# Where the tiles of x lie in SBUF: 2048 bytes apart in place of 2112, and one offset for the Strassen sums outside of them

## The chip, the core and the metric

The program runs on one core of a Trainium2 chip. The metric is the device time of one execution in microseconds (us). TensorE (PE in the profile) multiplies a stationary operand, loaded by LDWEIGHTS (PEld), with a moving operand that streams past it, and adds into PSUM. ScalarE (ACT) and VectorE (DVE) make its operands, SyncE (SP) issues most DMA transfers, GpSimd (POOL) does little here. SBUF is the on-chip memory of 128 partitions; an address below is a byte address inside each partition.

## The reference, cut to what matters

One decoder layer over 512 tokens of width 2048, batch 1, all in float32: a mixer of three head groups behind one input projection, cross-attention into 256 memory tokens, and a gated MLP (D_FF = 5504) with a causal depthwise convolution of width 3 on the gate. Before each stands an RMS norm, after each a residual add; a last RMS norm closes it.

```python
def hybrid_mixer(h, w_in, ...):
    proj = h @ w_in                       # (512, 2048) @ (2048, 6168)
    qa, ka, va, qb, kb, vb, fl, qc, kc, vc, rc, gl = jnp.split(proj, ...)
    o_a = dilated_mixture_attention(...)  # 12 heads of 64
    o_b = forgetting_attention(...)       # 8 heads of 64
    o_c = rms_norm(gla_chunked(...)) * jax.nn.silu(rc)
    return jnp.concatenate([o_a, o_b, o_c], axis=-1) @ w_out

def memory_cross_attention(h, mem_n, w_q, w_kv, w_o):
    ...                                   # 4 heads of 128, softmax over 256 memory tokens
    return o @ w_o

def conv_ffn(h, w_up, conv_w, conv_b, w_down):
    val, gate = jnp.split(h @ w_up, 2, axis=-1)
    g = conv_b
    for i in range(CONV_W):
        g = g + conv_w[i] * gp[:, i:i + S]
    return (jax.nn.silu(g) * val) @ w_down

def reference(x, mem, ...):
    mem_n = rms_norm(mem, mem_norm)
    for l in range(DEPTH):                # DEPTH = 1
        x = x + hybrid_mixer(rms_norm(x, norm_mix[l]), ...)
        x = x + memory_cross_attention(rms_norm(x, norm_cross[l]), mem_n, ...)
        x = x + conv_ffn(rms_norm(x, norm_ffn[l]), ...)
    return rms_norm(x, norm_final)
```

## The kernel before

Activations stand with features on the partitions and the 512 tokens along the row: 16 tiles of 128 x 512. Every float32 operand is split in two: ACT rounds it to fp32r ("hi"), DVE subtracts to get the rest ("lo"). A product is then three matmuls, hi with hi, lo of the moving operand with hi, hi with lo of the weights (`mm3`, lines 352 to 354). Weights come by DMA into `wraw` and are split into `whi` and `wlo`, tiles of 2048 bytes, of which a matmul takes 128 columns (512 bytes) as its stationary operand.

The work on PE goes stage by stage:

- the mixer's projections (`out_units`: the moving operand is a tile of x, 512 columns; `nat_units`, lines 393 to 395: the moving operand is a weight tile of 384, 408 or 512 columns, and 128 columns of a tile of x are the stationary one). After every 12 matmuls of `out_units`, `tick` may put in instructions of attention or of the gated linear attention, matmuls among them;
- the output projection `w_o`, the keys and values of the memory (`mhi`, `mlo`, 256 columns), and the cross-attention, whose output projection moves `coh` and `col` (512 columns);
- the up projection of the MLP, 43 rounds of seven Strassen products. Both factors are cut into quarters, so its moving operands are sums of quarters with 256 columns. `token_sums` makes 56 of them: eight pairs i = 0 to 7 by seven products. Each is one tile that holds hi (1024 bytes) and behind it lo (1024 bytes). A product runs over i = 0 to 7 in that order, three matmuls each, 24 in a row;
- the down projection: 43 tiles of the gate product g, 512 columns, of which some lie in the tiles of x (`xhi`, `xlo`) and some in tiles of their own (`gh`, `gl`, `gkh`, `gkl`); PE goes over them in blocks.

The tiles of x are 16 `xhi` and 16 `xlo` of the pool `xp` (`xslot`, line 292). They hold the normed x, then the mixed heads, then x again for the cross-attention, then the first 32 of the 56 sums (slots 0 to 31, that is i = 0 to 3 and four of i = 4), then tiles of g, then the last weights. The other 24 sums lie in pools of their own (`sx`, `fa`) and are named `sum32` to `sum55`.

Where they lie, in the program as built (the phase is the address modulo 512, since the slices of a weight tile stand 512 bytes apart):

| tiles | first address | distance | phase |
|---|---|---|---|
| whi, wlo | 32192, 42432 | 2048 | 448 |
| x tiles, before | 52672 | 2112 | 448, 0, 64, 128, ... (64 more each tile; `xhi` and `xlo` of one number have one phase) |
| mhi, mlo | 175040 | 1024 | 448 |
| coh, col | 153024 | 2048 | 448 |
| gh, gl | 168896, 189376 | 2048 | 448 |
| sum32 to sum48, before | 193408 | 2112 | 384, 448, 0, ... |
| sum49 to sum55, before | 153024 | 2112 | 448, 0, 64, ... |

Inside its tile a Strassen sum of pair i begins SHIFT[i] words behind the start: 0, 4, 8, 16, 24, 32, 48 or 56 bytes for i = 0 to 7. The order of the instructions is that of the code; pools place tiles one behind the other.

Of the kernel before, what the change touches and what calls it, by code (L numbers as in the profile page):

```python
# [13 lines left out]
F32R = mybir.dt.float32r  # L14
# [5 lines left out]
P = 128  # L20
D = 2048
KT = D // P
S = 512
# [22 lines left out]
FC = ((0, 5), (5, 10))  # L46
GX_SLOTS = 16
GB_SLOTS = 10
SHIFT = (0, 1, 2, 4, 6, 8, 12, 14)
LEVELS = (64, 32, 16, 8, 4, 2, 1)  # L50
A_PATTERNS = ((128, 1), (512, 4), (2048, 16))
REL_BUCKETS = 32
# [159 lines left out]
class _Trunk:  # L212
# [77 lines left out]
        return self.gains[:, i * KT + k:i * KT + k + 1]  # L290

    def xslot(self, n=S):
        hi = self.xp.tile([P, n], F32R, name="xhi", tag="xhi", bufs=KT, padded_shape=[P, S + 16])
        lo = self.xp.tile([P, n], F32R, name="xlo", tag="xlo", bufs=KT, padded_shape=[P, S + 16])
        return hi, lo

    def split(self, src, n=S):
# [835 lines left out]
    def token_sums(self, i, pool, tmp):  # L1133

        nc = self.nc
        y = []
        for e in range(2):
            t = tmp.tile([P, S], F32, name="y%d" % e, tag="y%d" % e, bufs=2)
            nc.scalar.activation(t, self.x1[2 * i + e], AF.Copy, scale=self.gain(2, 2 * i + e))
            y.append(t)  # L1140
        a11, a21 = y[0][:, :HT], y[0][:, HT:]
        a12, a22 = y[1][:, :HT], y[1][:, HT:]
        s = [tmp.tile([P, HT], F32, name="s%d" % n, tag="s%d" % n, bufs=2) for n in range(1, 5)]
        src = {1: a11, 6: s[1], 5: s[0], 7: s[2], 4: a22, 2: a12, 3: s[3]}
        made = {5: (a21, a22, ALU.add), 6: (s[0], a11, ALU.subtract), 7: (a11, a21, ALU.subtract),
                3: (a12, s[1], ALU.subtract)}
        out = {}
        for n, j in enumerate((1, 5, 6, 7, 4, 2, 3)):
            if j in made:
                nc.vector.tensor_tensor(src[j], made[j][0], made[j][1], op=made[j][2])  # L1150
            slot = 7 * i + n
            if slot < 2 * KT:
                tag = ("xhi", "xlo")[slot % 2]
                t = self.xp.tile([P, S + 16], F32R, name=tag, tag=tag, bufs=KT)
            else:
                t = pool.tile([P, S + 16], F32R, name="sum%d" % slot)
            o = SHIFT[i]
            th, tl = t[:, o:o + HT], t[:, o + HT:o + S]
            nc.scalar.activation(th, src[j], AF.Copy)  # L1159
            nc.vector.tensor_tensor(tl, src[j], th.bitcast(F32), op=ALU.subtract)  # L1160
            out[j] = (th, tl)
        return out
# [232 lines left out]
```

## Time and profile before

| | |
|---|---|
| time, median of 3 runs (lowest, highest) | 2411.97 us (2410.82, 2414.61) |
| profiled execution, its own time | 2413.33 us |
| its span from first to last instruction | 2411.5 us |
| PE busy | 2360.5 us (98%), 14514 matmuls |
| DVE busy, ACT busy | 1657.7 us (69%), 1140.8 us (47%) |
| DMA | 269.15 MB, 112 GB/s in the mean |
| mean granted TensorE clock | 0.991 of full speed |

Matmuls are pipelined: each one's own duration (about 390 ns for 512 columns) covers the two or three behind it, so what one costs is the distance between the starts of two that follow each other. Over a stretch in which PE is busy without a break it is the length of the stretch over the count, where one or two matmuls that began before the stretch's edge, or begin on its end, have to be taken off the count.

### The profile page before, as it was taken

To read this page: it belongs to the slowest core of one execution; us is meant where nothing else is said; L and a number is where in the kernel's file an instruction comes from. 1 tells how busy PE (TensorE), PEld (TensorE's weight loads), DVE (VectorE), ACT (ScalarE), POOL (GpSimd) and SP (SyncE) were. 2 spreads that over 40 slices of the span, in tenths; PEclk is the share of its full clock that TensorE was granted. 3 is DMA by queue.
4 is the path that set the end of the run, shared out by engine and by line. 5 is a ranking of instruction groups with operands and counts; after the bars stand their busy time and mean duration, and the time that the engine had idled before them with its cause. 6 is when DMAs were issued, how large, how long until landed. Compare 5 with 4: busy or idle time off the path is not lost.

```text
span 2411.5 us, 37909 instructions
## 1 busy us (share of the span) xinstructions
PE 2360.5 (98%) x14514; PEld 2119.6 (88%) x14514; DVE 1657.7 (69%) x3112; ACT 1140.8 (47%) x2185; POOL 88.2 (4%) x91
## 2 busy tenths in 40 slices
PE   9999999999999999889999999999999899999997
PEld 8798898888878888689999999999999788888887
DVE  7726656667785365888888888888888733343336
ACT  6323346555664264655555555555555522232223
POOL 2000000000001000100000000000000000000003
PEclk9999999999999999989999999999999999999999
DMA  6432132222224352123333333333333533242332
GB/s 206 145 95 83 47 105 80 96 89 94 86 91 149 119 161 80 60 94 119 119 119 119 119 119 119 119 119 119 119 119 119 184 104 120 96 158 96 109 103 73
DMA packets 87458, 269.15 MB, mean 112 GB/s; under 512 B 9788, under 2 KB 14540, under 8 KB 87276
## 3 DMA queue, kind: packets, MB, share of 16 engines
q1 hardware_dynamic: 79504, 254.64, 32.9%
q10 hardware_dynamic: 7772, 12.09, 1.5%
q8 instruction: 114, 1.87, 0.3%
q14 instruction: 68, 0.56, 0.1%
HBM read 251.18 MB, written 19.45 MB: 112 GB/s over the span
## 4 chain that ended last, share of the span: by engine, by line
PE 93%; DVE 3%; ACT 2%; DMA 1%; POOL 1%; issue 0%; DVEq 0%; SPq 0%; POOLq 0%; ACTq 0%
PE acc L352 18%; PE acc L354 18%; PE acc L353 18%; PE psC L353 3%; PE psC L352 3%; PE psC L354 3%; PE acc L393 3%; PE acc L395 3%; PE acc L394 3%; PE psD L353 2%; PE psD L354 2%; PE psD L352 2%; PE psU L354 2%; PE psV L354 2%; PE psU L353 2%; PE psV L353 2%
## 5 line engine op out<-in xcount | busy, mean ns | idle before, releaser
L339 DVE TENSOR_TENSOR wlo<-wraw,whi 128x512 fp32r<-128x512 f32 (+2 forms) x496 | 336.8, 683 | 427.4 <-ACT whi L338 418.8
L338 ACT ACTIVATE whi<-wraw 128x512 fp32r<-128x512 f32 (+2 forms) x496 | 304.5, 617 | 643.5 <-PE acc L353 381.9
L352 PE MATMUL acc<-xhi,whi 128*128 128x512 f32 (+1 forms) x1518 | 554.4, 365 | 14.8 <-ACT xhi L1258 9.0
L354 PE MATMUL acc<-xhi,wlo 128*128 128x512 f32 (+1 forms) x1518 | 548.8, 362 | 0.0
L353 PE MATMUL acc<-xlo,whi 128*128 128x512 f32 (+1 forms) x1475 | 535.7, 363 | 0.0
L352 PEld LDWEIGHTS acc<-xhi,whi 128*128 128x128 f32 x1518 | 286.8, 189 | 56.6 <-ACT xhi L1258 9.2
L354 PEld LDWEIGHTS acc<-xhi,wlo 128*128 128x128 f32 x1518 | 287.4, 189 | 46.0 <-issue 0.8
L353 PEld LDWEIGHTS acc<-xlo,whi 128*128 128x128 f32 x1475 | 278.8, 189 | 43.5 <-issue 0.9
L313 ACT ACTIVATE whi<-wraw 128x512 fp32r<-128x512 f32 x344 | 215.7, 631 | 201.2 <-PE acc L353 70.3
L314 DVE TENSOR_TENSOR wlo<-wraw,whi 128x512 fp32r<-128x512 f32 x344 | 232.3, 686 | 34.0 <-ACT whi L313 32.7
L313 ACT ACTIVATE whi<-t 128x512 fp32r<-128x512 f32 x258 | 162.9, 633 | 160.2 <-PE acc L353 97.0
L314 DVE TENSOR_TENSOR wlo<-t,whi 128x512 fp32r<-128x512 f32 x258 | 173.5, 687 | 40.0 <-ACT whi L313 39.2
L352 PE MATMUL acc<-sum,whi 128*128 128x256 f32 x559 | 157.8, 282 | 0.9 <-ACT sum L1159 0.9
L353 PE MATMUL acc<-sum,whi 128*128 128x256 f32 x559 | 157.9, 283 | 0.5 <-DVE sum L1160 0.5
L354 PE MATMUL acc<-sum,wlo 128*128 128x256 f32 x559 | 157.3, 281 | 0.0
L353 PE MATMUL acc<-xhi,whi 128*128 128x256 f32 x430 | 121.6, 283 | 0.0
L393 PE MATMUL acc<-whi,xhi 128*128 128x384 f32 (+2 forms) x320 | 114.8, 359 | 1.0 <-ACT whi L338 0.6
L395 PE MATMUL acc<-whi,xlo 128*128 128x384 f32 (+2 forms) x320 | 112.6, 352 | 0.4 <-DVE xlo L306 0.4
L394 PE MATMUL acc<-wlo,xhi 128*128 128x384 f32 (+2 forms) x320 | 112.3, 351 | 0.0
L352 PE MATMUL acc<-xlo,whi 128*128 128x256 f32 x387 | 109.5, 283 | 0.0
L354 PE MATMUL acc<-xlo,wlo 128*128 128x256 f32 x387 | 109.3, 282 | 0.0
L353 PEld LDWEIGHTS acc<-sum,whi 128*128 128x128 f32 x559 | 106.0, 190 | 0.7 <-DVE sum L1160 0.7
(369 smaller groups left out, 5245.0 us busy)
## 6 DMA issues: line engine op xcount, KB each, us to landing
wraw<-in_w_up SPq DMA_DIRECT2D x172, 512.0 KB, 3.8
wraw<-in_w_dn SPq DMA_DIRECT2D x80, 512.0 KB, 3.7
wraw<-in_w_o SPq DMA_DIRECT2D x32, 512.0 KB, 3.6
wraw<-in_w_qka SPq DMA_DIRECT2D x24, 512.0 KB, 3.7
gd<-cv SPq DMA_DIRECT2D x43, 256.0 KB, 4.3
graw<-gd SPq DMA_DIRECT2D x43, 256.0 KB, 4.4
wraw<-in_w_qkb SPq DMA_DIRECT2D x16, 512.0 KB, 3.8
xraw<-in_xT SPq DMA_DIRECT2D x15, 512.0 KB, 3.8
```

The lines of the kernel that those rows point to most:

```text
L313: nc.scalar.activation(hi, r, AF.Copy)
L314: nc.vector.tensor_tensor(lo, r, hi.bitcast(F32), op=ALU.subtract)
L338: nc.scalar.activation(hi, r, AF.Copy)
L339: nc.vector.tensor_tensor(lo, r, hi.bitcast(F32), op=ALU.subtract)
L352: nc.tensor.matmul(out, lh, rh, start=start, stop=False, skip_group_check=more)
L353: nc.tensor.matmul(out, lh, rl, start=False, stop=False, skip_group_check=more)
L354: last = nc.tensor.matmul(out, ll, rh, start=False, stop=stop, skip_group_check=more)
L393: self.nc.tensor.matmul(o, xh[:, tt], wh, start=(k == 0), stop=False)
L394: self.nc.tensor.matmul(o, xh[:, tt], wl, start=False, stop=False)
L395: self.last = self.nc.tensor.matmul(o, xl[:, tt], wh, start=False, stop=(k == KT - 1))
```

## The change

The padding of the tiles of x goes: they are 2048 bytes long and stand 2048 bytes apart. Sums that lie in them start at the tile's start, whatever i; sums outside keep their tiles of 2112 bytes and all begin 32 bytes (SHIFT = 8 words) behind the start.

```diff
-SHIFT = (0, 1, 2, 4, 6, 8, 12, 14)
+SHIFT = 8
...
     def xslot(self, n=S):
-        hi = self.xp.tile([P, n], F32R, name="xhi", tag="xhi", bufs=KT, padded_shape=[P, S + 16])
-        lo = self.xp.tile([P, n], F32R, name="xlo", tag="xlo", bufs=KT, padded_shape=[P, S + 16])
+        hi = self.xp.tile([P, n], F32R, name="xhi", tag="xhi", bufs=KT, padded_shape=[P, S])
+        lo = self.xp.tile([P, n], F32R, name="xlo", tag="xlo", bufs=KT, padded_shape=[P, S])
...
             if slot < 2 * KT:
                 tag = ("xhi", "xlo")[slot % 2]
-                t = self.xp.tile([P, S + 16], F32R, name=tag, tag=tag, bufs=KT)
+                t, o = self.xp.tile([P, S], F32R, name=tag, tag=tag, bufs=KT), 0
             else:
-                t = pool.tile([P, S + 16], F32R, name="sum%d" % slot)
-            o = SHIFT[i]
+                t, o = pool.tile([P, S + 16], F32R, name="sum%d" % slot), SHIFT
```

In the program as built, all 32 tiles of x then have phase 448. The pools that stood behind `xp` on the left side (`mc`, `mab`, `ox`, `fa`) move down by 2048 bytes, so their phases stay. Sums 32 to 48 begin at phases 416, 480, 32, ... (64 more each), sums 49 to 55 at 480, 32, 96, ... No instruction is added or taken away, and on every engine they stand in the order of before. One wait moves: of the first reloads of g (line 1250 before), the wait for a matmul of the up projection goes from the second to the third, since the sums in `fa` lie lower.

## Rows read from the trace of the kernel before

**Rows 1.** The page: busy time, share of the span and instructions of each engine; then the chain that ended last, by engine.

```profile
PE 2360.5 (98%) x14514; PEld 2119.6 (88%) x14514; DVE 1657.7 (69%) x3112; ACT 1140.8 (47%) x2185; POOL 88.2 (4%) x91
...
PE 93%; DVE 3%; ACT 2%; DMA 1%; POOL 1%; issue 0%; DVEq 0%; SPq 0%; POOLq 0%; ACTq 0%
```

**Rows 2.** Who PE waited for: us in total, times, longest. The longest four.

```profile
PE acc L352 <- ACT xhi L1258: 9.0, 1, 9.0
PE acc L354 <- DVE wlo L339: 6.6, 3, 3.1
PE acc L352 <- ACT whi L313: 6.3, 2, 5.8
PE acc L352 <- ACT xhi L1159: 3.7, 2, 3.1
```

**Rows 3.** Busy time of PE in stretches: stretch, its length, PE busy (instructions), granted clock, DMA share, GB/s. In this order: a block of gh and gl in the down projection, from its seventh matmul on; the output projection w_o (x tiles); a block of x tiles in the down projection; the memory's keys (mhi, mlo, 256 columns); the Strassen products.

```profile
2134.51:2150.60 16.09, 16.09 (x72) 1.00 0.30 95
...
712.54:800.61 88.07, 88.07 (x382) 1.00 0.42 139
1972.23:1994.49 22.26, 22.26 (x98) 1.00 0.30 96
862.98:877.37 14.39, 14.39 (x121) 1.00 0.61 183
1049.10:1894.00 844.90, 844.90 (x7088) 1.00 0.38 119
```

**Rows 4.** PE in order of time where the down projection goes over from tiles of x to gh and gl: start and duration in us, line, operation, out<-operands (moving one first), shape.

```profile
2132.89 0.39 PE L354 MATMUL psV<-xhi,wlo 128*128 128x512 f32 x1
2133.12 0.39 PE L352 MATMUL psU<-gh,whi 128*128 128x512 f32 x1
...
2134.51 0.39 PE L352 MATMUL psU<-gh,whi 128*128 128x512 f32 x1
2134.73 0.39 PE L353 MATMUL psU<-gl,whi 128*128 128x512 f32 x1
```

**Rows 5.** Groups of PE instructions in three stretches, by line, names and shape: count, busy us, mean ns of one. First the down projection (1903 to 2360 us), then 702 to 1032 us, then the mixer (46 to 702 us).

```profile
L353 PE MATMUL acc<-xlo,whi 128*128 128x512 f32 x240 | 95.6, 398 | 0.0
...
L353 PE MATMUL psU<-xlo,whi 128*128 128x512 f32 x120 | 47.3, 394 | 0.0
...
L353 PE MATMUL psV<-xlo,whi 128*128 128x512 f32 x120 | 47.2, 394 | 0.0
...
L353 PE MATMUL acc<-xlo,whi 128*128 128x512 f32 x272 | 106.5, 392 | 0.0
...
L353 PE MATMUL acc<-xlo,whi 128*128 128x512 f32 x545 | 215.7, 396 | 0.0
L393 PE MATMUL acc<-whi,xhi 128*128 128x384 f32 x192 | 66.3, 345 | 0.0
...
L393 PE MATMUL acc<-whi,xhi 128*128 128x512 f32 x64 | 26.0, 406 | 0.0
```

**Rows 6.** PE in order of time in the mixer, where attention puts transposes between the projection's matmuls.

```profile
453.98 0.82 PE L531 MATMUL psT<-ident,pt 128*128 128x128 f32 x6
454.56 0.48 PE L352 MATMUL acc<-xhi,whi 128*128 128x512 f32 x1
454.87 0.39 PE L353 MATMUL acc<-xlo,whi 128*128 128x512 f32 x1
...
457.18 0.40 PE L354 MATMUL acc<-xhi,wlo 128*128 128x512 f32 x1
457.41 1.03 PE L531 MATMUL psT<-ident,pt 128*128 128x128 f32 x8
```

**Rows 7.** PE in order of time in one Strassen product: the first matmul of the triples i = 0 (no offset), i = 1 (4 bytes), i = 2 and i = 3.

```profile
1501.75 0.28 PE L352 MATMUL psC<-xhi,whi 128*128 128x256 f32 x1
...
1502.10 0.28 PE L352 MATMUL psC<-xlo,whi 128*128 128x256 f32 x1
...
1502.47 0.28 PE L352 MATMUL psC<-xhi,whi 128*128 128x256 f32 x1
...
1502.83 0.28 PE L352 MATMUL psC<-xlo,whi 128*128 128x256 f32 x1
```

**Rows 8.** PE in order of time at the start of the memory's keys: the first matmul of that block and its thirteenth.

```profile
862.98 0.28 PE L352 MATMUL acc<-mhi,whi 128*128 128x256 f32 x1
...
864.41 0.28 PE L352 MATMUL acc<-mhi,whi 128*128 128x256 f32 x1
```

**Rows 9.** SP's queue in order of time at the end of the up projection: the store of the last gate product, then the reloads of g; and PE's first matmul behind it.

```profile
1910.19 0.33 SPq L1232 DMA_DIRECT2D gd<-cv  x1
1910.57 5.28 SPq L1250 DMA_DIRECT2D graw<-gd  x9
...
1914.16 0.80 PE L352 MATMUL acc<-xhi,whi 128*128 128x512 f32 x1 [8.99 <-ACT xhi L1258]
```

**Rows 10.** Busy time of every engine in the stretch of the Strassen products: length, then PE, PEld, DVE, ACT, POOL busy (instructions), clock, DMA share, GB/s.

```profile
1060.00:1915.00 855.00, 846.01 (x7095) 845.36 (x7093) 752.82 (x1145) 457.33 (x767) 0.00 (x0) 1.00 0.38 120
```

## The prediction

> **What bounds the kernel now.** I read the page first. The reader is to see that PE is busy for 98% of the span and carries 93% of the chain that ended last [rows 1]. Then the waits: PE's four longest come to 25.6 us in all, at stage boundaries [rows 2]. So the time is the count of matmuls times what one costs, and the change moves no instruction; it can act only through the cost of a matmul. Then the busy time by stretches, with the distance from one start to the next in each: a stretch over its count, less the matmuls on its edges [rows 3]. The down projection shows what matters. With gh and gl as moving tiles a matmul of 512 columns costs 16.09 us / 71 = 226.6 ns; with tiles of x, on the same lines, of the same shape, in the same stage, 22.26 / 96 = 231.9 ns; in w_o, tiles of x again, 88.07 / 381 = 231.2 ns [rows 3]. Both are at the full granted clock. What differs is where the tiles lie. gh and gl stand 2048 bytes apart at phase 448, the phase of every weight slice; the tiles of x walk by 64 bytes each. The order of time shows how the short distance is reached: after a block of x the first six matmuls on gh and gl still cost (2134.51 - 2133.12) / 6 = 232 ns, then 0.22 to 0.23 us [rows 4]. The cost depends on what went before, and a constant phase settles on the shorter one within about six matmuls.
>
> **The change part by part.** It brings the tiles of x to phase 448, as gh and gl have it. All sums are against the profiled execution's own 2413.33 us (span 2411.5 us and 1.8 us around it); the median of the runs shown is 1.36 us lower, and I take that off at the end.
>
> *Down projection.* Its matmuls on tiles of x are three groups of 240 and six of 120 (one line of each kind is shown): 1440 [rows 5]. Each goes from 231.9 to 226.6 ns: 1440 x 5.3 ns = 7.6 us. The blocks alternate between tiles of x and gh, now of one phase, so nothing has to settle anew.
>
> *Output projection and queries.* 702 to 1032 us has 3 x 272 = 816 matmuls on tiles of x, 512 columns [rows 5]. They run nearly unbroken [rows 3]; I let them settle at 227.3 ns, a little over the 226.6, for interruptions: 816 x 3.9 ns = 3.2 us.
>
> *Mixer.* 3 x 545 = 1635 such matmuls [rows 5], but broken by other matmuls: between the transposes at 453.98 and those at 457.41 us there are only twelve [rows 6]. If six of twelve pay the unsettled price, as in rows 4, half gain: 1635 / 2 x 4.6 ns = 3.8 us. The ends are 0 (never settled) and 7.5 us (all).
>
> *Weights as the moving operand.* Here the tiles of x are the stationary side. The 192 of 512 columns would gain as above, 192 x 4.6 ns = 0.9 us; the 576 of 384 columns [rows 5] and the 192 of 408 have no row at one phase, so I bound them by 2 ns either way, 1.5 us, and take 0.
>
> *Strassen products.* The largest block: 43 x 56 x 3 = 7224 matmuls, 844.90 us / 7086 = 119.2 ns each [rows 3]. 43 x 32 x 3 = 4128 of them move a tile of x. Two rows stand on either side. One triple without an offset takes 1502.10 - 1501.75 = 0.35 us, 116.7 ns each, the next, with 4 bytes, 0.37 us, 123.3 ns [rows 7]. Against that, mhi and mlo are this very case, 256 columns, hi and lo 1024 bytes apart, all of phase 448, and over 120 in a row they cost 14.39 / 120 = 119.9 ns [rows 3]. So one phase is worth nothing at 256 columns in the long run. In a product the tiles of x come 12 or 15 in a row before the sums outside; the first twelve of the memory's block took (864.41 - 862.98) / 12 = 119.2 ns [rows 8], just what the products cost now. That is the nearest row: no change for the 4128. For the 3096 outside, offsets of 24, 48 and 56 bytes become 32; I allow 0.3 ns, 1 us of gain. The ends for all 7224 are 116.7 ns, a gain of 18 us, and 119.9 ns, a loss of 5.1 us.
>
> Here the Trainium skill has a rule (SBUF — State Buffer, Specifications): lines of 16 bytes, and every step to a new line has a price. By it offsets of 4, 8, 24 and 56 bytes cost one line more in 64, an estimate of 1.9 ns in 119.2, and taking them out of half the sums would give about 6.7 us. The triple with 4 bytes in rows 7 is longer, as the rule has it, but by 20 ns where one line in 64 would be some 6 ns for three; the sum above does without it.
>
> *What costs nothing.* The moved wait: the reloads of g stand in SP's queue behind a store issued at 1910.19 us, which waits for the last gate product, while PE has stood still since 1914.16 - 8.99 = 1905.17 us [rows 9]; the matmul that was waited for is long past in either place. ACT and DVE write the same sizes; DVE is busy for 752.82 of 855 us in the Strassen stretch [rows 10], so PE could run over a tenth faster before DVE became the bound. The waits of rows 2 hang on DMA, ACT and DVE and stay.
>
> Sum: 7.6 + 3.2 + 3.8 + 0.9 + 1.0 = 16.5 us. 2413.33 - 16.5 = 2396.8 in terms of the profiled execution, 2395.5 us in terms of the median.
>
> **The rivals.** *Placement does not matter.* Then gh is faster for another reason, say since its tiles are few, and the time stays at 2412 us. For it: the memory's tiles have one phase and no advantage. Against it: rows 3 and 4, the same lines and shapes a few us apart. The Trainium skill speaks for this rival (SBUF — State Buffer, Who interferes with whom): the moving operand and LDWEIGHTS have read ports of their own, and PE never waits on anyone. By that rule 2412 us; the 5.3 ns in rows 3 disagree.
>
> *The Strassen products gain as well.* Were every triple as short as the one without offset, 116.7 ns, the 18 us take the place of the 1 us above: 2395.5 - 17 = 2378 us. Half of it, some in the tiles of x alone, gives 2387. For it: the first triple of rows 7. Against it: rows 8 and the memory's 119.9.
>
> *The Strassen products lose.* Place: the 24 matmuls of each product, where 12 to 15 of phase 448 alternate with sums 32 bytes off. If that keeps the stream at the slow triple's 123.3 ns [rows 7], the price is 7224 x 4.1 = 29.6 us, and with the other 15.5 us of gain the time is 2426 us. It decides for slower once the mean of the stage passes 119.2 + 15.5 / 7.224 = 121.3 ns. For it: rows 4 show that a change of phase costs about six matmuls, and here it comes twice in 24. Against it: now the phase changes with every triple, and the mean is 119.2.
>
> *The shorter distance is never reached in the mixer.* Then its 3.8 us go, 2399 us: inside the range.
>
> **How the numbers follow.** The forecast with its own range of 2388 to 2406 has 0.74; placement without effect 0.08; the Strassen gain 0.11; the Strassen loss 0.07. What a measurement of this kernel can tell from no change is about 0.2%, 4.8 us, so faster means under 2407.1 us: all of the forecast and the Strassen gain, 0.85. Of the loss I give 0.06 to slower and 0.01 to a size that just cancels the gain, so no change has 0.09. The range runs from 2384 (the forecast with two thirds of the Strassen gain) to 2407 (the mixer at 0, the Strassen products at 119.9 ns and a little more).
>
> **What would show it.** Right: in the down projection blocks on xhi and xlo come to 226 to 228 ns like those on gh; w_o to about 227; in the mixer the twelve matmuls between two interruptions start at 232 ns and end near 227; the Strassen stretch lies within 118.3 and 120 ns. Wrong: tiles of x still at 231 in the down projection (placement is not the cause), or a Strassen stretch outside of 118 to 121 ns, which by its 7224 matmuls outweighs all the rest: one ns there is 7.2 us.

## The result and the profile after

The changed kernel takes 2396.43 us in the median of 4 runs (2392.99 to 2397.52), the one before 2412.41 us on the same chip (4 runs, 2410.82 to 2414.61). The ratio is 0.9931, its 95% interval 0.9913 to 0.9948: 16 us faster, where 16.5 were predicted. The profiled execution took 2396.3 us.

The page first: span, busy time, share and count.

```profile
span 2394.5 us, 37907 instructions
...
PE 2342.9 (98%) x14514; PEld 2117.8 (88%) x14514; DVE 1657.9 (69%) x3112; ACT 1139.9 (48%) x2185; POOL 87.6 (4%) x91
```

The counts are those of [rows 1], DVE and ACT are busy as long as before, and PE is busy 17.6 us less; the span is 17.0 us shorter. So the same matmuls cost less. Who PE waited for (us in total, times, longest) answers to [rows 2]:

```profile
PE acc L352 <- ACT xhi L1257: 9.0, 1, 9.0
PE acc L354 <- DVE wlo L339: 6.4, 4, 3.1
PE acc L352 <- ACT whi L313: 5.5, 1, 5.5
PE acc L352 <- ACT xhi L1158: 3.7, 2, 3.1
PE acc L352 <- ACT sum L1158: 2.6, 2, 2.2
```

The four long waits are nearly as they were (9.0, 6.4, 5.5 and 3.7 us against 9.0, 6.6, 6.3 and 3.7). A fifth has grown: at the entry to the up projection PE waits 2.6 us for the sums. In the kernel before, where that line is 1159, it was 0.9 us:

```profile
PE acc L352 <- ACT sum L1159: 0.9, 1, 0.9
```

Now PE by stretches (stretch, length, busy time and count, granted clock, DMA share, GB/s), as in [rows 3]: a block of x tiles in the down projection (96 matmuls), a block of gh and gl (78), w_o (368), the memory's keys (120), the Strassen products.

```profile
1961.61:1983.37 21.76, 21.76 (x97) 1.00 0.30 98
2119.37:2137.05 17.68, 17.68 (x79) 1.00 0.34 115
711.39:794.82 83.43, 83.43 (x369) 1.00 0.44 146
856.07:870.46 14.39, 14.39 (x121) 1.00 0.61 183
...
1050.00:1880.00 830.00, 830.00 (x6993) 1.00 0.38 120
```

A row of 512 columns lasts 0.39 us and so reaches over one later start, not two or three, and one of 256 columns, 0.28 us, over two. Less the one on the edge of each, x tiles now cost 21.76 / 96 = 226.7 ns (231.9 before), gh and gl 17.68 / 78 = 226.7, w_o 83.43 / 368 = 226.7 (231.2), the memory's keys 119.9 as before, and the Strassen products 830 / 6992 = 118.7 (119.2).

PE in order of time (start, duration, line, operation): twelve matmuls of the mixer behind transposes and the next twelve, two of the first Strassen products (for the last section), and the passage from x to gh in the down projection:

```profile
444.77 0.47 PE L352 MATMUL acc<-xhi,whi 128*128 128x512 f32 x1
445.08 0.39 PE L353 MATMUL acc<-xlo,whi 128*128 128x512 f32 x1
...
447.14 0.39 PE L353 MATMUL acc<-xlo,whi 128*128 128x512 f32 x1
447.37 0.39 PE L354 MATMUL acc<-xhi,wlo 128*128 128x512 f32 x1
447.60 0.39 PE L518 MATMUL psS<-kh,qs 128*128 128x512 f32 x1
...
448.52 0.39 PE L352 MATMUL acc<-xhi,whi 128*128 128x512 f32 x1
...
451.24 0.81 PE L531 MATMUL psT<-ident,pt 128*128 128x128 f32 x6
...
1037.64 0.41 PE L352 MATMUL acc<-xlo,whi 128*128 128x256 f32 x1
...
1042.34 0.41 PE L354 MATMUL psC<-xlo,wlo 128*128 128x256 f32 x1
...
1983.15 0.39 PE L354 MATMUL acc<-xhi,wlo 128*128 128x512 f32 x1
1983.37 0.39 PE L352 MATMUL acc<-gh,whi 128*128 128x512 f32 x1
1983.60 0.39 PE L353 MATMUL acc<-gl,whi 128*128 128x512 f32 x1
...
1984.05 0.39 PE L352 MATMUL acc<-gh,whi 128*128 128x512 f32 x1
```

The six slow matmuls of [rows 4] are gone: from x to gh every third start is 0.68 us on. Behind transposes (128 columns) the twelve shown still begin long, (447.60 - 445.08) / 11 = 229 ns in the mean, and end at 0.23 us. Behind four matmuls of the attention, of 512 columns themselves, they are here short from the first, (451.24 - 448.52) / 12 = 226.7 ns. Over all 76 unbroken twelves of the mixer, 6.4 in the mean are over before the distances stay between 225 and 228.5 ns.

Where the time went, by group, from the distances between starts summed over the trace:

| group | predicted, us | before, us | after, us | change |
|---|---|---|---|---|
| down projection, x tiles | -7.6 | 330.96 | 323.68 | -7.3 |
| w_o and queries, x tiles | -3.2 | 189.26 | 186.10 | -3.2 |
| mixer, x tiles | -3.8 | 394.42 | 390.04 | -4.4 |
| weights moving, 512 columns | -0.9 | 45.21 | 44.77 | -0.4 |
| weights moving, 384 columns | 0 | 102.88 | 101.85 | -1.0 |
| gh, gl | not counted | 109.40 | 108.80 | -0.6 |
| coh, col | not counted | 61.42 | 60.47 | -1.0 |
| Strassen products, undisturbed | -1.0 | 119.17 ns each | 118.73 ns each | -3.2 |

(The last is 0.44 ns x 7224.) That is 21 us. The 1.0 us of coh and col do not come from their placement, since their phase is the same: 14 of their 192 matmuls start 0.43 us apart, at a granted clock of 0.50 (1.2 GHz), where before it was 17. Against the 21 us stand 0.4 us on the weights of 408 columns, 0.3 us on the last products of the down projection, the 1.7 us of the longer wait for the sums, and small change elsewhere; 17.0 us of span are left. By stages, from first matmul to first matmul, the trace is 4.2 us shorter up to w_o and 4.0 from there to the up projection; the first hundred matmuls of the up projection, with the wait for the sums, take 1.6 us longer; the rest of it takes 3.1 us less, and the down projection 7.5.

### The profile page after: what moved, and what is told of

Its sections match the earlier page's. It is cut to its first block, busy times and chain, and to the rows that moved or that the text cites. A ratio compares the mean times of both kernels' runs of the same rounds, so it can differ in the third digit from the quotient of the medians.

```text
span 2394.5 us, 37907 instructions
## 1 busy us (share of the span) xinstructions
PE 2342.9 (98%) x14514; PEld 2117.8 (88%) x14514; DVE 1657.9 (69%) x3112; ACT 1139.9 (48%) x2185; POOL 87.6 (4%) x91
## 4 chain that ended last, share of the span: by engine, by line
PE 93%; DVE 4%; ACT 1%; POOL 1%; DMA 0%; issue 0%; DVEq 0%; SPq 0%; POOLq 0%; ACTq 0%
PE acc L354 18%; PE acc L353 18%; PE acc L352 18%; PE psC L352 3%; PE psC L353 3%; PE psC L354 3%; PE acc L395 3%; PE acc L393 3%; PE acc L394 3%; PE psD L354 2%; PE psD L352 2%; PE psD L353 2%; PE psV L353 2%; PE psU L353 2%; PE psU L354 2%; PE psV L354 2%
## 5 line engine op out<-in xcount | busy, mean ns | idle before, releaser
L314 DVE TENSOR_TENSOR wlo<-wraw,whi 128x512 fp32r<-128x512 f32 x344 | 232.0, 685 | 32.9 <-ACT whi L313 32.4
```

Source lines behind the costliest of these rows:

```text
L314: nc.vector.tensor_tensor(lo, r, hi.bitcast(F32), op=ALU.subtract)
```

## The experiments

Below, "mean" is the mean distance between starts: for 512 columns that of the x tiles in the down projection, without those that an interruption stretches; for the Strassen products over all from the hundredth of the stage on. Two theories stood at the start. A: only a phase that stays the same from matmul to matmul counts. B: moving tile and weight slice must have one phase. A third, C, came after the run with 64 bytes ahead of x: what the stream settles on is set by the difference of the two phases. Every run with no range beside it was measured once. The rival that placement does not matter had fallen with the windows above.

### Each half of the change alone

**The distance alone**: the changed kernel with the old offsets for the sums outside of x.

```diff
-SHIFT = 8
+SHIFT = (0, 1, 2, 4, 6, 8, 12, 14)
...
-                t, o = pool.tile([P, S + 16], F32R, name="sum%d" % slot), SHIFT
+                t, o = pool.tile([P, S + 16], F32R, name="sum%d" % slot), SHIFT[i]
```

> The first half of the change alone: tiles of x 2048 bytes apart, sums in them at the tile's start, sums outside with their offsets of before (24 to 56 bytes by pair). Theory: all the gain of the 512-column matmuls as in the kernel after (226.7 ns settled), Strassen matmuls in tiles of x 119.0 ns, those outside 118.3 to 118.9, time 2396 to 2399 us: of the 8 us that the offsets alone brought, hardly any is left once the tiles of x have one phase. Rival (the two halves add): 2404 us, so that the whole change owes 8 us to the offsets.

Measured: 2400.48 us (2398.62 to 2401.04) against 2414.71 before, ratio 0.9941 (0.9926 to 0.9955). The whole gain of the 512-column matmuls is there, mean 226.7 ns; the Strassen products rise to 119.40 ns, 0.23 x 7224 = 1.7 us more than before. That is more than expected, and so is the time: the sums outside of x stand at 119.4 ns, not at 118.3 to 118.9. In the whole time this run and the changed kernel can't be told apart (the intervals of their ratios overlap); in the Strassen stage they can, 119.40 against 118.73 ns.

**The offsets alone**: the kernel before, 2112 bytes apart, its sums in x without offset and those outside with 32 bytes.

```diff
-SHIFT = (0, 1, 2, 4, 6, 8, 12, 14)
+SHIFT = 8
...
-                t = self.xp.tile([P, S + 16], F32R, name=tag, tag=tag, bufs=KT)
+                t, o = self.xp.tile([P, S + 16], F32R, name=tag, tag=tag, bufs=KT), 0
...
-                t = pool.tile([P, S + 16], F32R, name="sum%d" % slot)
-            o = SHIFT[i]
+                t, o = pool.tile([P, S + 16], F32R, name="sum%d" % slot), SHIFT
```

> The kernel before with the second half of the change alone: sums in tiles of x without offset, sums outside with 32 bytes, tiles of x still 2112 bytes apart. By the theory the 512-column matmuls stay at 231 to 232 ns, and the Strassen matmuls lose only the offsets of 4, 8, 24 and 56 bytes: 119.2 falls to 118.3 to 119.0 ns, 1 to 6 us, time 2406 to 2411 us. Rival (the offsets carry the gain): below 2402 us.

Measured: 2403.17 us, against 2411.14 before: 8 us, more than expected, from one run of each. The 512-column matmuls stay at 231.8 ns. The Strassen stretch, the same window for the two halves, here the distance alone:

```profile
1050.00:1880.00 830.00, 830.00 (x6954) 1.00 0.37 119
```

and the offsets alone:

```profile
1050.00:1880.00 830.00, 830.00 (x7053) 1.00 0.38 120
```

The first has 830 / 6953 = 119.4 ns, the second 830 / 7052 = 117.7; the changed kernel, with both, 118.7. The halves do not add: the offsets alone are worth 1.5 ns x 7224 = 10.9 us in this stage, and with tiles of x at one phase 7.7 us of that are lost. The place is in the tiles of x: 117.38 ns in this kernel, 119.03 in the changed one, x 4128 = 6.8 us. (The span of this trace, 2401.3 us, is 10.2 us under that of the kernel before, so 8 and 10.9 us are nearer to each other than they seem.)

### Which phase counts

**256 bytes ahead of the tiles of x**: they then have phase 192, the weights still 448.

```diff
+        gap = es.enter_context(tc.tile_pool(name="gap", bufs=1))
+        gap.tile([P, 64], F32, name="gap")
```

> The kernel after, with 256 bytes left free ahead of the tiles of x: all of them have phase 192 (address mod 512) and stand 2048 bytes apart, weight slices stay at 448. Theory A (what counts is that the phase stays the same from matmul to matmul): 512-column matmuls on tiles of x in the down projection and in w_o cost 226.7 to 227.5 ns as in the kernel after, time 2396 +- 4 us, except where blocks of gh (448) and x alternate. Theory B (moving tile and weight slice must have one phase): they go back to 231 ns and above, time 2410 +- 4 us.

Measured: 2393.83 us (before, there: 2412.29). Block of x tiles in the down projection:

```profile
1958.99:1980.74 21.75, 21.75 (x97) 1.00 0.29 97
```

21.75 / 96 = 226.6 ns, and the Strassen products at 118.73 ns as in the changed kernel. No cost moved, which could mean A or a period of 256 bytes.

**256 bytes between the xhi and the xlo**: their phase now alternates between 448 and 192.

```diff
+        self.apart = None
...
+        if not self.apart:
+            self.apart = self.xp.tile([P, 64], F32, name="gap")
```

> The kernel after, with 256 bytes left free between the 16 xhi and the 16 xlo: hi at phase 448, lo at phase 192, neighbours of a kind still 2048 bytes apart. Theory A (the phase must stay the same from one matmul to the next): it changes twice in three matmuls now, so 512-column matmuls on tiles of x cost 229 to 236 ns, time 2404 to 2425 us. Rival (the distance of 2048 bytes between neighbours is what counts): 226.7 ns, time 2396 +- 4 us. Theory B (one phase with the weights): hi stays short, lo does not, about 228 to 230 ns in the mean.

Measured: 2395.06 us, x tiles 226.7 ns, Strassen products 118.73. The 229 to 236 ns of A did not come. Either an alternation of 256 bytes is none at all, since the period divides 256, or only the distance between neighbours of one kind counts; the runs with 64 and 128 bytes between xhi and xlo below decide for the first. The unit of 512 in the prediction, and so the run ahead of this one, was too coarse to tell the theories apart.

**64 bytes ahead of the tiles of x** (the `gap` above with 16 words). In this run and the next two, what lies behind the gap on the same side, coh, col and sums 49 to 55 among it, moves with it.

> The kernel after, with 64 bytes left free ahead of the tiles of x: all of them at phase 0 (mod 512), weight slices at 448, distances as in the kernel after. 256 bytes changed nothing, so 256 is a whole number of periods and that run did not tell theories A and B apart; 64 bytes are not, since in the kernel before steps of 64 cost 231 ns. Theory A (the phase must only stay the same from matmul to matmul): 226.7 to 227.5 ns on tiles of x in w_o, a few matmuls at 230 ns at each change between tiles of x and gh in the down projection, time 2396 to 2400 us. Theory B (moving tile and weight slice must have one phase): 229 ns and more throughout, time 2404 us and more.

Measured: 2396.69 us (before: 2411.14). w_o, 368 matmuls of x tiles:

```profile
711.16:795.38 84.22, 84.22 (x369) 1.00 0.43 145
```

84.22 / 368 = 228.9 ns, in the down projection 229.7. A falls. The 229 ns and more that B had on record are met or nearly met, its 2404 us are not: the Strassen products gain, to 117.97 ns, 5.5 us, which pays for the loss and puts the time in the range of A for another reason. The distances in w_o come round in threes, near 226, 229 and 232 ns: a steady phase settles, on a cost that depends on the difference to the weights, as C has it. Unforeseen: the last products of the down projection (256 columns, gkh and gkl moving, x tiles as weights; start, duration, line, operation as above):

```profile
2363.55 0.28 PE L354 MATMUL psD<-gkh,xhi 128*128 128x256 f32 x1
...
2365.93 0.28 PE L354 MATMUL psD<-gkh,xhi 128*128 128x256 f32 x1
```

These are 21 matmuls apart, 113.3 ns each, and 113.4 in the mean of all, where the changed kernel has 120.0.

**64 bytes between the xhi and the xlo** (the tile above with 16 words).

> The kernel after, with 64 bytes left free between the 16 xhi and the 16 xlo: hi at phase 448, lo at 0, so the phase changes by 64 twice in three matmuls. Theories A and B: 512-column matmuls on tiles of x cost 229 to 236 ns, time 2404 to 2425 us. Rival (only the step from one k to the next counts, as the kernel before had it between triples): 226.7 ns, 2396 us.

Measured: 2407.74 us. w_o, 381 matmuls:

```profile
710.06:798.46 88.40, 88.40 (x382) 1.00 0.41 139
```

88.40 / 381 = 232.0 ns, in the down projection 231.9. A moving tile whose phase changes from matmul to matmul loses the whole 512-column gain, though only half of the tiles have moved, and by 64 bytes. The difference to the weights alone does not give that: xlo moves in one matmul of three, and with the 229.7 ns of the run before for these and 226.7 for the others the mean would be an estimated 227.7. The change itself costs.

**128 bytes between them** (32 words).

> As the run with 64 bytes between xhi and xlo, with 128 bytes. If the phase counts modulo 128, nothing changes: 226.7 ns, 2393 to 2397 us. If it counts modulo 256: 229 to 236 ns, 2404 to 2425 us.

Measured: 2402.59 us. w_o, 381 matmuls:

```profile
711.71:800.58 88.87, 88.87 (x382) 1.00 0.41 137
```

88.87 / 381 = 233.3 ns, in the down projection 229.5. So 128 is no period: it is 256. In w_o the distances come round as 230, 235, 235 ns, in the down projection as 226, 227, 234: with the same phases the stream settles on two different cycles, which no run explains. The time lies 1.4 us under what was expected; the Strassen products, at 118.29 ns, are shorter than in the changed kernel.

### What the Strassen products settle on

**All sums at one phase**: those outside of x in tiles of 2048 bytes and without offset, all 56 at 448.

```diff
-                t, o = pool.tile([P, S + 16], F32R, name="sum%d" % slot), SHIFT
+                t, o = pool.tile([P, S], F32R, name="sum%d" % slot), 0
```

> The kernel after, with the 24 Strassen sums outside the tiles of x at phase 448 too, without offset and 2048 bytes apart: all 56 sums have one phase. Theory A (one phase throughout settles on the count of columns plus 32 cycles: 288 cycles, 120.0 ns for 256 columns): the Strassen matmuls go from 118.7 to 120.0 ns, 7224 x 1.3 ns = 9 us longer, time 2405 +- 3 us. Rival (one phase is good for every shape, 32 bytes of offset cost something): the sums outside get shorter, under 118.3 ns, time 2388 to 2396 us.

Measured: 2404.62 us. The Strassen stretch:

```profile
1050.00:1880.00 830.00, 830.00 (x6919) 1.00 0.37 119
```

830 / 6918 = 120.0 ns, and every matmul from the hundredth on lies at 120, as was expected: the value on which the memory's keys stood [rows 3]. At 256 columns the phase of the weights is the slowest of those tried.

**The same tiles, other pairs**: x holds the sums of pairs 0, 2, 4, 6 and four of 5 in place of 0 to 3 and four of 4, so that tiles of one phase come in shorter runs.

```diff
+        self.turn = 0
...
-            if slot < 2 * KT:
-                tag = ("xhi", "xlo")[slot % 2]
+            if i in (0, 2, 4, 6) or (i == 5 and n < 4):
+                tag = ("xhi", "xlo")[self.turn % 2]
+                self.turn += 1
```

> The kernel after, with the same tiles given to other pairs: pairs 0, 2, 4, 6 and four sums of pair 5 lie in tiles of x, the others outside, so that within a product tiles of x and sums outside alternate from pair to pair. Theory A (256-column matmuls settle on 120.0 ns only after some ten at one phase, and are shorter before): the runs of 120.0 ns vanish, the Strassen mean falls from 118.7 to about 118.0 ns, 5 us shorter, time 2391 +- 4 us. Rival (every change of phase costs): more changes, mean above 119.2 ns, time 2400 us or more.

Measured: 2389.28 us, 7 us under the changed kernel's median. The Strassen stretch:

```profile
1050.00:1880.00 830.00, 830.00 (x7007) 1.00 0.37 120
```

830 / 7006 = 118.5 ns, half a nanosecond over what was expected: 0.24 x 7224 = 1.7 us of the 7. So the time came out as expected, but not for the reason expected. Most of the rest, some 4 us, lies at the entry to the up projection: the long wait for the sums is gone from PE's list, and that for xhi on line 1158 with it; a part of it may be the order in which the sums are made. With one run that stays open.

**The weights of the up projection 64 bytes on**: all 56 sums at 448 as above, the weight slices 64 bytes behind the start of longer tiles (the other tiles of that pool grow with them).

```diff
-        hi = self.wp.tile([P, n], F32R, name="whi", tag="whi", bufs=WS, padded_shape=[P, 512])
-        lo = self.wp.tile([P, n], F32R, name="wlo", tag="wlo", bufs=WS, padded_shape=[P, 512])
+        hi = self.wp.tile([P, 576], F32R, name="whi", tag="whi", bufs=WS)[:, 16:16 + n]
+        lo = self.wp.tile([P, 576], F32R, name="wlo", tag="wlo", bufs=WS)[:, 16:16 + n]
...
```

> All 56 sums at phase 448 as in the run that settled on 120.0 ns, and for the Strassen products the weight slices 64 bytes behind their tile's start (tiles 2304 bytes apart, so that every slice has phase 0 modulo 256 and moving less stationary is -64). Theory C (what a matmul settles on is set by the difference of the two phases modulo 256): as in the last products of the run with the tiles of x moved by 64 bytes, where the weights had that difference and 256 columns took 113.4 ns: 7224 x (118.7 - 113.4) = 38 us less than the kernel after, time 2355 to 2364 us, the upper end if VectorE, 88% busy in that stage, begins to hold PE up. Rival (113.4 ns belongs to those products, not to the difference): 117 to 120 ns, time 2385 to 2406 us.

Measured: 2388.44 us (2386.5 to 2389.75), ratio 0.9891 (0.9877 to 0.9905): faster than both kernels. The Strassen stretch:

```profile
1050.00:1880.00 830.00, 830.00 (x7050) 1.00 0.38 121
```

830 / 7049 = 117.7 ns (117.78 in the mean), steady between 117 and 119. The 113.4 ns that the run with 64 bytes ahead of x showed in its last products, at the same difference of phases, did not come: the expectation built on it missed by 24 us or more, so C as it stood, with the difference as the only cause, falls for 256 columns.

**The same with 32 and with 128 bytes** (`[:, 8:8 + n]` and `[:, 32:32 + n]`).

> The same with 32 bytes. If the cost falls with the distance: about 118.9 ns, 8 us over the run with 64, time about 2396 us. If any difference is alike: 117.8 ns, 2388 +- 3 us. If only steps of 64 count: 120.0 ns, 2404 us.

> As the run with the weight slices of the Strassen products 64 bytes behind, with 128 bytes, the half period. Differences of 0, +64 and -64 settled on 120.0, 117.8 and 117.8 ns. If the cost falls with the distance of the two phases, 128 bytes come below 117.8 ns (115.5 by a straight line, the Strassen products 16 us shorter than at 64, time about 2372 us). If any difference that is not 0 is alike, 117.8 ns, 2388 +- 3 us. If the half period meets the same trouble as 0, 120 ns and 2404 us.

Measured: with 32 bytes 2390.61 us (2390.32 to 2392.1), ratio 0.9908 (0.9891 to 0.9924), 118.33 ns; with 128 bytes 2394.41 us (2392.0 to 2405.9), ratio 0.9933 (0.9908 to 0.9958), 118.67 ns. The Strassen stretch with 32 bytes, then with 128:

```profile
1050.00:1880.00 830.00, 830.00 (x7016) 1.00 0.38 120
...
1050.00:1880.00 830.00, 830.00 (x6997) 1.00 0.37 120
```

With the run at one phase that makes a series for the Strassen products, by the distance of the weights from the moving tiles: 0 bytes 120.0, 32 bytes 118.3, 64 bytes 117.8, 128 bytes 118.7 ns. None of the costs expected for 32 and 128 bytes came. And only 0 and 64 bytes settle: with 32 the distances spread from 115 to 123 ns, with 128 from 114 to 123, so those two figures are means of an uneven stream.

## Why the prediction was right

**Down projection, 7.6 us: 7.3 measured.** gh and gl served as the measure for x, and both now stand at 226.7 ns. That it is the placement and no other trait of gh is shown by 64 bytes between xhi and xlo, which bring 231.9 back. The Trainium skill (SBUF — State Buffer, Who interferes with whom) has PE wait on nobody, with read ports of their own for the moving operand and LDWEIGHTS. Here 226.7 against 231.9 ns for the same matmuls, 64 bytes apart in the placement of half of their moving tiles, are a price that this rule has no place for; the traces do not show what it is that waits.

**w_o and queries, 3.2 us: 3.2 measured.** The 227.3 ns assumed came out at 227.2 over the whole group, without the distances that an interruption stretches.

**Mixer, 3.8 us: 4.4 measured.** Half of the matmuls were to gain, for six of twelve pay the old price after a break. It took 6.4 of twelve: behind transposes three to ten, most often seven, behind attention's matmuls of 512 columns none in four passages of six. With the shorter passages a little over half of the gain was reached. That the count came out is in part luck: the six were read off one passage from x to gh, where the phase itself changed.

**Weights as the moving operand, 0.9 us: 1.0 measured**, but otherwise spread: 0.4 on the 512 columns, 1.0 on the 384, which was taken as 0 within 1.5, and 0.4 lost on the 408.

**Strassen products, 1.0 us: 3.2 in the matmuls.** 118.7 ns lies within the 118.3 to 120 that were named. The step "no change for the 4128" rested on the first twelve of the memory's block at 119.2; they came to 119.03 from 119.55. So the 3096 outside gave what was predicted, 0.34 ns or 1.1 us, and the 4128, put at nothing, gave 2.1. The 116.7 and 123.3 ns of [rows 7] were those of one product: over 286 products of that trace the triple i = 0 takes 117.8 ns a matmul and i = 1 120.6. And the 4128 were no standing still: the distance alone costs 1.7 us here, the offsets alone give 10.9, and what was measured is neither of the two nor their sum. The prediction had no row for the offsets without the distance and allowed 0.3 ns for them; its bound of 116.7 held.

The Trainium skill's lines of 16 bytes (SBUF — State Buffer, Specifications) gave an estimate of 6.7 us for taking the offsets of 4, 8, 24 and 56 bytes out of the sums. The run with the offsets alone gave 8 us, of that order; but the run without any offset, all sums at phase 448, is the slowest of all in this stage, 120.0 ns, and moving the weights alone by 64 bytes gives 117.8. A price per line has no place for that.

**What costs nothing.** The moved wait did cost nothing: the wait ahead of the down projection is 9.0 us in both. The waits as a whole did not quite stay: the 1.7 us more at the sums, whose cause no run isolates.

**The sum.** The 16.5 us are close to the 17.0 of span and 16.0 of the medians partly by luck. The matmuls gave some 20 us through their placement, 3 to 4 more than the sum has, most of it in the Strassen products, in the mixer and in groups taken as 0; the longer wait for the sums and small losses elsewhere, which the sum put at nothing, took about as much away.

**The rivals.** "Placement does not matter" fell with the first window. "The Strassen products gain as well" did not come, but the run with the offsets alone shows 10.9 of its 18 us, at 117.7 ns, in reach; "they lose" came at its most with all sums at one phase, at 120.0 (the distance alone has 119.4), below the 121.3 ns that would have decided. The mixer did reach the shorter distance.

One premise was wrong without harm: phases were taken modulo 512, since slices stand 512 bytes apart; the runs with 256 bytes show that 256 is enough. At 2048 bytes both give the same.

## What to carry to other kernels

Where a profile shows PE busy throughout, compare the distance between the starts of matmuls of one shape across stages: 2% between two sets of tiles on the same line was worth 14 us here, and tiles of 512 columns that stood a multiple of 256 bytes apart, at the phase of the weight slices, took the shorter one. That rule does not carry over to 256 columns, where the same placement was the slowest, and 64 bytes between weights and moving tiles the best of the four distances tried with all moving tiles at one phase. And where a change has two halves, time each alone: here one gave 14 us, the other 8 (one run), both together 16.

## What was not expected of the hardware

Where moving tiles and weights have one phase, the settled distances are exact: at the full granted clock, 2.4 GHz, 226.67 ns for 512 columns are 512 + 32 cycles, 120.0 ns for 256 columns 256 + 32. At the lower level of the clock the 32 are not seen: in the first products of the up projection, behind PE's waits there, starts lie (1042.34 - 1037.64) / 22 = 213.6 ns apart (the two rows at 1037.64 and 1042.34 us in the order of time above), and 256 cycles of 1.2 GHz are 213.3. The stretches, with PE alone, show the clock, 0.50:

```profile
1030.00:1040.00 10.00, 4.24 (x18) 0.50 0.15 52
...
1041.00:1042.00 1.00, 1.00 (x7) 0.50 0.00 0
```

The period of 256 bytes was not expected either, nor that at 256 columns the cost is lowest with the weights 64 bytes off, of the distances tried, and not with them as far off as can be. Open is what it is that collides (the traces show only the distance), why the products of 256 columns ran at 113.4 ns in one place and at 117.8 in another with the same difference of phases, why 128 bytes between xhi and xlo cost more in w_o than in the down projection, and whether the shorter waits with the other pairs would hold in further runs.
